# Attention's side work, places for weights and the order of sevens changed in a decoder layer

## The chip, the cores and the metric

The kernel runs on one core of a Trainium2 chip. The metric is the time of one execution on the device in microseconds (us); smaller is better. Engines are named as in the profile: PE (TensorE), DVE (VectorE), ACT (ScalarE), POOL (GpSimd) and SP (SyncE, which here only issues DMAs).

## The reference

One decoder layer over 256 tokens of width 2048, all in float32:

```
x = layer_norm(alpha*x + 0.5*swiglu(x, f1_gu, f1_down))         # feed-forward 1, inner width 5632
mixed = gated(retention(...), sliding_window_attention_sinks(...)) @ w   # token mixers
x = layer_norm(alpha*x + mixed)
x = layer_norm(alpha*x + 0.5*swiglu(x, f2_gu, f2_down))         # feed-forward 2
x = layer_norm(alpha*x + gated per-layer embedding)

def swiglu(x, w_gu, w_down):
    g, u = jnp.split(x @ w_gu, 2, axis=-1)
    return (jax.nn.silu(g) * u) @ w_down
```

The attention has 16 query heads of 64 over 4 key heads, a window of 128 keys, and for each head a learned sink logit in the softmax's denominator. Its gates and inputs come from the columns of one large matrix w_in.

## The kernel before

Every matrix product takes its weights from the chip's memory in chunks of 512 KB and is done in three matmuls: weight and activation are split into a high and a low part, and high x low, high x high and low x high are added (L431, L432, L433). ACT casts the high part of a weight (L105, names with h: hf_gu), DVE subtracts it from the raw one (rf_gu) and so makes the low part (L106, lf_gu). A *unit* is a pair of chunks with the matmuls that use them, of one of these kinds:

- P, plain: 24 matmuls.
- F, Folded: plain, but the low part is made by an accumulating DMA which POOL issues (L170).
- S, a *seven*: seven products of sums of sub-blocks in the place of eight, 21 matmuls. DVE makes the sums u and v of the weights (L226 to L229), ACT and DVE split them (huf, luf, hvf, lvf), and at the end of a block DVE folds the seven products into the results (L541 to L544, in the down product L1059 behind them). The sums of the activations are the *forms* (seven_forms; gaf0 and gaf1 in the gates' part).
- D, Prepared: a seven whose u and v were computed and put in memory earlier, so that it loads six tiles (huf, luf, hvf, lvf, and raw tiles) at once.

All these tiles come from one pool of 46 places (SLOTS). fill(), which is called whenever a unit is done, loads the next unit of the plan or makes the loaded one, if the number of places that slots_for_weights last set is not used up and if less than 90 (far) or 45 (ahead) matmuls are queued in the units at hand. A place count thus decides how long before its use a transfer is issued. Each engine takes its instructions in the order in which the program emits them; SP issues its DMAs in that order too and waits at one whose tile isn't free yet.

Feed-forward 2 computes gate and up in 11 blocks of 512 columns (f20 to f210; loads are named rf2_gu_block_half_number in the order and rf_gu in the profile). The down product has a first and a second half of output columns, each with 22 units whose kinds stand in FIRST_DOWN and SECOND_DOWN; feed-forward 1 uses the same tables. At the end of the second half stand the additions to the residual (L1118) and the layer norm (L646 to L706; lnps at L684 is its transpose on PE).

The attention's scores, softmax and products run as *side work*: side is a list of steps, one of which is run after each chunk of the feature groups (4 chunks each: aqk, akv) and of the gate projection gt (32 chunks of 12 matmuls). For head pair m a step holds one or more parts: att1 (scores as on PE; mask and maxima on DVE), att1b (exponentials on ACT, L1412), att1c (normalising on DVE, L1426), att2 (cutting into wat on ACT, L185), att2a (transposing DMA to mat), att2b (joining into apt on ACT, L201), att3 (ao on PE, L1454, and attt on ACT and DVE). In the profile and the text "head" is such a pair. The list begin holds the step at which head m starts.

Of the kernel before, what the change touches and what calls it, by code (L numbers as in the profile page):

```python
# [9 lines left out]
F32R = mybir.dt.float32r  # L10
# [6 lines left out]
P = 128  # L17
# [24 lines left out]
SEVEN = (0, 1, 2, 3)  # L42

AHEAD = {1: (4, 5), 2: (4,), 3: (4, 5), 4: (4,), 5: (4, 5), 7: (4, 5)}
AHEAD_SLOTS = 32

DELAY = 1

SEVEN_DOWN = (6, 7, 8, 9)

FIRST_DOWN = "PPPPPPFFSFSPSFSPSFSSPS"
SECOND_DOWN = "PPPSPSPSFSPSFSPSPSPPPP"
LEAD = 4

BIG = 3.0e38
# [7 lines left out]
def layer(ctx: ExitStack, tc: tile.TileContext, io):  # L63
# [13 lines left out]
    def banks(name):  # L77
        return [bank(name + str(j)) for j in range(2)]

    def slot(shape, dt, name):  # L80
        return slots.tile(shape, dt, tag="slot", name=name)
# [22 lines left out]
    def split(dst_hi, dst_lo, src, lo_engine=None):  # L104
        act.copy(dst_hi, src)  # L105
        (lo_engine or dve).tensor_tensor(dst_lo, src, dst_hi, ALU.subtract)  # L106
# [249 lines left out]
    def slots_for_weights(n, ahead=45, far=90):  # L356
        room.update(slots=n, ahead=ahead, far=far)
# [136 lines left out]
            if p == sevens[-1]:  # L494
                fold(p1.ap, p6.ap, p7.ap, q5.ap)

    def seven_forms(full, hi, lo, between=None):


        a11, a21 = (full[:, 0::2, t * P : (t + 1) * P] for t in range(2))  # L500
        a12, a22 = (full[:, 1::2, t * P : (t + 1) * P] for t in range(2))
        raw = slot([P, 8, P], F32, "sums")
        f5, f6, f7, f3 = (raw[:, 2 * j : 2 * j + 2, :] for j in range(4))
        dve.tensor_tensor(f5, a21, a22, ALU.subtract)
        dve.tensor_tensor(f7, a11, a21, ALU.subtract)
        dve.tensor_tensor(f6, f5, a11, ALU.subtract)
        dve.tensor_tensor(f3, a12, f6, ALU.add)
        if between is not None:
            between()
        split(hi, lo, raw)  # L510
        return lambda e: [(hi[:, 2 * j + e, :], lo[:, 2 * j + e, :]) for j in range(4)]

    def whole(parts, name):

        full = slot([P, 4, S], F32, name)
        n = 4 // len(parts)
        for j, v in enumerate(parts):
            dve.tensor_tensor(full[:, n * j : n * j + n], v[:, :, :S], v[:, :, S:], ALU.add)
        return full

    def forms_of(parts, name):
        hi, lo = (slot([P, 8, P], F32R, name + w) for w in "hl")
        return seven_forms(whole(parts, name + "w"), hi, lo)
# [338 lines left out]
    ht = big.tile([P, KD, 512], F32R, tag="ht", name="xt")  # L862

    def load_constants():
        act.dma_start(cst, io["cst"])
        act.dma_start(mask, io["mask"])
        act.dma_start(gn, io["gn"])
        act.dma_start(sink, io["att_sinks"].broadcast_to([P, HA]))
# [44 lines left out]
    def gu_units(name, j):  # L913
        if j == 0:
            return [("P", p) for p in range(KD // 2)]
        if name == "f2" and j in AHEAD:
            plain = "P" if j < 4 else "F"
            return units_of(*((f"P{plain}SDSDSP", SEVEN[:3]) if j % 2 else (f"P{plain}SSDSSP", SEVEN)), AHEAD[j])
        order = "FFSSFSSP" if name == "f1" or j > 8 else "PFSSFSSP"
        return units_of(order, SEVEN[: order.count("S")])  # L920

    def gu_keys(name, j):
        return lambda n, p: (name + "_gu", j, n, p)

    def down_units(n_held):
# [4 lines left out]
        first, second = [], []  # L930
        for out, order in ((first, FIRST_DOWN), (second, SECOND_DOWN)):
            n = order.count("S")
# [17 lines left out]
    def ffn(name, i, ht, norm, keep, residual, keepers, away):  # L950
# [4 lines left out]
        made = {}  # L955
# [25 lines left out]
        def convert(g):  # L981
            convert_high(g)()

        for j in range(KF // 4):
            pg, pu = banks(f"{name}g{j}"), banks(f"{name}u{j}")
            units = gu_units(name, j)
            n_of = {(0, 0): KD, (0, 1): KD, (1, 0): KD, (1, 1): KD}
            for kind, p in units:
                if kind in "SD":
                    for at in ((0, 0), (0, 1), (1, 0)):  # L990
                        n_of[at] -= 1
                    n_of[1, 1] -= 2
            sums = [[Sum((pg, pu)[n][t], n_of[t, n]) for n in range(2)] for t in range(2)]
            got = []

            if norm is not None and j == 0:
                front, units = units[:FRONT_PAIRS], units[FRONT_PAIRS:]
                steps = [(gu_keys(name, 0)(n, p), 2 * p, n) for _, p in front for n in range(2)]
                norm.first(steps, rhs, sums, (
                    (3, (1, 0)), (5, "more"), (5, (1, 1)), (7, (0, 2)), (8, (1, 2)), (9, (0, 3)), (10, (1, 3)), (10, "go"),  # L1000
                ))
                slots_for_weights(24)

            def before(u, j=j, offset=KD // 2 - len(units)):
                u += offset
                if j == 0 and norm is None and u % 2 == 0:
                    first_chunk(u // 2)
                    if u == 6:
                        slots_for_weights(24)
                    if u == 2:  # L1010
                        load_constants()
                if j == 0 and u == 7:
                    for g in sorted({p // 2 for p in SEVEN}):
                        hi, lo = (slot([P, 8, P], F32R, f"{name}f{w}{g}") for w in "hl")
                        made[g] = seven_forms(keep[g], hi, lo)
                    if name == "f2":
                        g = AHEAD[1][0] // 2
                        made[g] = forms_of([ht[:, 4 * g : 4 * g + 4, :]], f"{name}f{g}")
                if name == "f2" and j in AHEAD and u == 0:
                    slots_for_weights(AHEAD_SLOTS - j)  # L1020
                if j == KF // 4 - 1 and u in (4, 6):
                    convert(u // 2 - 2)

            block(f"{name}{j}", units, gu_keys(name, j), rhs, forms, sums, lambda *a: got.extend(seven_common(*a)), before)
            if got:
                g, v = got
                for x, ps in ((g, pg), (v, pu)):
                    for t in range(2):
                        dve.tensor_tensor(x[:, t], x[:, t], ps[t], ALU.add)
                act.activation(g, g, AF.Silu)  # L1030
                dve.tensor_tensor(v, g, v, ALU.mult)
            else:
                v = slot([P, 2, 512], F32, f"{name}v{j}")
                for t in range(2):
                    act.activation(v[:, t], pg[t], AF.Silu)
                for t in range(2):
                    dve.tensor_tensor(v[:, t], v[:, t], pu[t], ALU.mult)
            later(1, lambda j=j, v=v: turned(j, v))
# [9 lines left out]
        made = {}  # L1048
# [38 lines left out]
        sums = [[Sum(pn[n][t], n_of[0][t, n]) for n in range(2)] for t in range(2)]  # L1087
# [24 lines left out]
        sums = [[Sum(pt_[t][n], n_of[1][t, n]) for n in range(2)] for t in range(2)]  # L1112
# [74 lines left out]
    def mixers(ht, norm, residual, keepers, away):  # L1187
# [31 lines left out]
        sums = [[Sum(ps[t], KD)] for t in range(2)]  # L1219
# [4 lines left out]
        for c in range(FRONT, KD // 2):  # L1224
            u = take(("w_rv", 0, c))
# [17 lines left out]
        grp = 8  # L1243
# [9 lines left out]
        keep = {}  # L1253
# [92 lines left out]
        for h in range(0, HR, 2):  # L1346
# [3 lines left out]
            g = slot([P, 2, 512], F32, f"rgs{h}")  # L1350
# [3 lines left out]
            c = h // 2  # L1354
# [14 lines left out]
            dst = akv[:, 0:2, :] if j == 4 else aq[j // 2][:, j % 2 * 2 : j % 2 * 2 + 2, :]  # L1369
            rotate(ps, f"ra{j}", dst, *trig["a"], SH_A)  # L1370

        for grp in (20, 16, 17):
            attention_features(grp)
        assert not side

# [87 lines left out]
            return f  # L1463


        begin = [0, 5, 10, 15, 20, 24, 28, 32, 38, 39]
        at = [[] for _ in range(40)]
        for m in range(8):
            for j, part in ((0, att1), (1, att1b), (2, att1c), (3, att2), (4, att2a), (6, att2b)):
                at[begin[m] + j].append(part(m))  # L1470
            at[begin[m + 2]].append(att3(m))
        side.extend((lambda jobs=jobs: [f() for f in jobs]) for jobs in at)

        for grp in (18, 19):
            attention_features(grp)

        made = {}
# [2 lines left out]
        sig = []  # L1480
        for j in range(4):
            def before(c, j=j):
                if c == 0 and j >= 2:
                    g = j - 2
                    made[g] = forms_of([ht[:, 4 * g : 4 * g + 4, :]], f"gaf{g}")

            ps = banks(f"gt{j}")
            paired_out(("w_in_f2", 21 + 2 * j), KD, rhs, ps, before)
            sig.append(slot([P, 2, 512], F32, f"sig{j}"))
            for t in range(2):  # L1490
                (act.copy if j < 2 else dve.tensor_copy)(sig[-1][:, t], ps[t])
# [41 lines left out]
        for b in range(2):  # L1533
# [3 lines left out]
            for n in range(2):  # L1537
                j = 2 * b + n
# [37 lines left out]
        sums = [[Sum(ps[t], KD)] for t in range(2)]  # L1576
# [3 lines left out]
        for c in range(first):  # L1580
            u = take(("w_mix", 3, c))
# [147 lines left out]
    def first_chunk(c):  # L1729

        if c == 0:
            load_x_chunk(0)
            fill()
        if c < 3:
            load_x_chunk(c + 1)
# [157 lines left out]
```

## Time and profile before

| what | value |
|---|---|
| median of 3 runs | 2248.59 us (2248.32 to 2249.66) |
| the profiled execution | 2250.32 us, span 2248.5 us |
| PE busy | 2230.2 us (99%) |
| DVE busy | 1987.0 us (88%) |
| ACT busy | 1421.7 us (63%) |
| mean granted clock of PE | 0.997 |
| transfers issued by SP (queue q1) | 530.16 MB, 70.5% of 16 engines' span |

Busy time is the sum of the durations of an engine's instructions; a wait is the time that an engine stood ahead of an instruction, with what it stood for. In a timeline row the first number is the start, the second the duration, and the brackets hold the idle time ahead of it and what ended that. The granted clock is the share of full speed that the throttle let TensorE have.

### The profile page before, as it was taken

What the parts mean: (1) busy time and instruction counts of PE and PEld (TensorE: products, weight loads), DVE (VectorE), ACT (ScalarE), POOL (GpSimd) and SP (SyncE); (2) the same over time, 40 slices, a digit from 0 to 9 for tenths busy, and PEclk for the clock granted to TensorE, in tenths of its full rate; (3) what the DMA queues carried; (4) which work ended last, traced back from release to release, by engine and by line L of the source; (5) the groups of instructions that cost most, each with busy time, mean ns of one, the idle gap of its engine ahead of it and who ended that gap; (6) DMA issues with size and microseconds to landing.
All of it is one profiled execution on the core that took longest, in us unless ns stands there. A gap on an engine that the chain in (4) does not pass through costs nothing.

```text
span 2248.5 us, 29078 instructions
## 1 busy us (share of the span) xinstructions
PE 2230.2 (99%) x10173; PEld 1846.2 (82%) x10173; DVE 1987.0 (88%) x2601; ACT 1421.7 (63%) x1662; POOL 51.7 (2%) x66
## 2 busy tenths in 40 slices
PE   9999999999999999999999999999999999999998
PEld 8888888888888888888778888888888788888877
DVE  6999999989988898888789778789999899999877
ACT  6777777776554544656766466466667577765533
POOL 0000000000000000000000000000000000000000
PEclk9999999999999999999999999999999999999999
DMA  9989998977686899855657578888889799676872
GB/s 323 252 261 253 248 262 246 266 214 233 235 302 253 304 324 315 272 167 184 197 169 244 165 240 300 299 278 289 309 272 289 254 251 275 207 238 225 290 267 71
DMA packets 294283, 564.48 MB, mean 251 GB/s; under 512 B 92268, under 2 KB 96748, under 8 KB 294136
## 3 DMA queue, kind: packets, MB, share of 16 engines
q1 hardware_dynamic: 283944, 530.16, 70.5%
q0 software_dynamic: 8208, 29.89, 7.1%
q10 hardware_dynamic: 1984, 2.58, 0.4%
q8 instruction: 80, 1.31, 0.2%
q14 instruction: 67, 0.55, 0.1%
HBM read 484.43 MB, written 29.36 MB: 229 GB/s over the span
## 4 chain that ended last, share of the span: by engine, by line
PE 90%; DVE 4%; DMA 3%; issue 2%; ACT 1%; ACTq 0%; POOL 0%; DVEq 0%; POOLq 0%
PE rqk L382 3%; PE f1g L431 3%; PE f1g L432 3%; PE f1g L433 3%; PE f2g L431 2%; PE f2g L432 2%; PE f2g L433 2%; PE f1u L433 2%; PE f1u L431 2%; PE f1u L432 2%; PE f2u L433 2%; PE f2u L431 2%; PE f2u L432 2%; PE aqk L382 2%; PE f1d L433 1%
## 5 line engine op out<-in xcount | busy, mean ns | idle before, releaser
L106 DVE TENSOR_TENSOR lf_gu<-rf_gu,hf_gu 128x1024 fp32r<-128x1024 f32 (+1 forms) x225 | 267.7, 1210 | 21.3 <-ACT hf_gu L105 20.5
L105 ACT CAST hf_gu<-rf_gu 128x1024 fp32r<-128x1024 f32 (+1 forms) x225 | 228.7, 1040 | 35.9 <-DMA rf_gu<-in_f_gu 31.9
L106 DVE TENSOR_TENSOR lw_in_f<-rw_in_f,hw_in_f 128x1024 fp32r<-128x1024 f32 x140 | 167.9, 1220 | 29.8 <-ACT hw_in_f L105 29.8
L106 DVE TENSOR_TENSOR lf_down<-rf_down,hf_down 128x1024 fp32r<-128x1024 f32 x130 | 155.5, 1220 | 14.5 <-ACT hf_down L105 13.9
L105 ACT CAST hf_down<-rf_down 128x1024 fp32r<-128x1024 f32 x130 | 132.8, 1049 | 38.3 <-DMA rf_down<-in_f_down 26.9
L105 ACT CAST huf_gu<-uf_gu 128x1024 fp32r<-128x1024 f32 x76 | 80.1, 1054 | 121.2 <-DVE uf_gu L227 104.0
L105 ACT CAST hw_in_f<-rw_in_f 128x1024 fp32r<-128x1024 f32 x140 | 140.8, 1048 | 8.4 <-PE rv L432 3.2
L105 ACT CAST hvf_gu<-vf_gu 128x1024 fp32r<-128x1024 f32 x76 | 80.1, 1054 | 32.0 <-DVE vf_gu L229 30.2
L106 DVE TENSOR_TENSOR luf_gu<-uf_gu,huf_gu 128x1024 fp32r<-128x1024 f32 x76 | 92.7, 1219 | 0.0
L106 DVE TENSOR_TENSOR lvf_gu<-vf_gu,hvf_gu 128x1024 fp32r<-128x1024 f32 x76 | 92.6, 1219 | 0.0
L431 PE MATMUL f1g<-hf_gu,xt 128*128 128x512 f32 x232 | 90.9, 392 | 0.0
L432 PE MATMUL f1g<-hf_gu,xt 128*128 128x512 f32 x232 | 90.6, 390 | 0.0
L433 PE MATMUL f1g<-lf_gu,xt 128*128 128x512 f32 x232 | 90.5, 390 | 0.0
L431 PE MATMUL f2g<-hf_gu,ht 128*128 128x512 f32 x214 | 83.7, 391 | 0.0
L433 PE MATMUL f2g<-lf_gu,ht 128*128 128x512 f32 x214 | 83.5, 390 | 0.0
L432 PE MATMUL f2g<-hf_gu,ht 128*128 128x512 f32 x214 | 83.5, 390 | 0.0
L433 PE MATMUL f1u<-lf_gu,xt 128*128 128x512 f32 x192 | 74.9, 390 | 0.8 <-DMA lf_gu<-rf_gu 0.8
L170 POOL DMA_DIRECT2D lf_gu<-rf_gu x43 | 37.2, 866 | 1657.5 <-DMA rf_gu<-in_f_gu 1021.6
L431 PE MATMUL f1u<-hf_gu,xt 128*128 128x512 f32 x192 | 74.7, 389 | 0.0
L432 PE MATMUL f1u<-hf_gu,xt 128*128 128x512 f32 x192 | 74.7, 389 | 0.0
L105 ACT CAST huf_down<-uf_down 128x1024 fp32r<-128x1024 f32 x32 | 33.7, 1053 | 57.2 <-DVE uf_down L227 55.2
L433 PE MATMUL f2u<-lf_gu,ht 128*128 128x512 f32 x168 | 65.5, 390 | 0.4 <-DMA lf_gu<-rf_gu 0.4
(1469 smaller groups left out, 6914.7 us busy)
## 6 DMA issues: line engine op xcount, KB each, us to landing
rf_gu<-in_f_gu SPq DMA_DIRECT2D x360, 512.0 KB
rf_down<-in_f_down SPq DMA_DIRECT2D x176, 512.0 KB
rw_in_f<-in_w_in_f SPq DMA_DIRECT2D x148, 512.0 KB
lf_gu<-rf_gu POOLq DMA_DIRECT2D x43, 512.0 KB, 7.5
rw_rv<-in_w_rv SPq DMA_DIRECT2D x32, 512.0 KB
rw_ret<-in_w_ret SPq DMA_DIRECT2D x32, 512.0 KB
rw_mix<-in_w_mix SPq DMA_DIRECT2D x32, 512.0 KB
rw_pg<-in_w_pg SPq DMA_DIRECT2D x32, 512.0 KB
```

Source lines behind the costliest of these rows:

```text
L105: act.copy(dst_hi, src)
L106: (lo_engine or dve).tensor_tensor(dst_lo, src, dst_hi, ALU.subtract)
L170: pool.dma_start(c.lo, c.raw, accum_op=ALU.add)
L382: pe.matmul(ps[f], hi[:, kk, f * P : (f + 1) * P], rhs(k), start=k == 0, stop=k == n_k - 1,)
L431: pe.matmul(o, al, bh, start=first, stop=False)
L432: pe.matmul(o, ah, bh, start=False, stop=False)
L433: pe.matmul(o, ah, bl, start=False, stop=self.left == 0)
```

## The change

Four things change, with the same instructions on every engine:

- In feed-forward 2 the places for weights in blocks 1 to 10 become 36 less the block's number, in every block. Before they were 32 less the number in the blocks of AHEAD (1, 2, 3, 4, 5, 7) and stayed as they were in the others.
- In SECOND_DOWN the last S stands at place 16 in the place of 17 (counted from 0), and two pairs of S are neighbours.
- The attention's side work begins with feature group 17 in the place of 18, over 44 steps in the place of 40, and the parts of one head stand at other distances from its start: 0, 2, 3, 4, 5, 7 in the place of 0, 1, 2, 3, 4, 6. ao of the last head stays in the last step.
- The forms of the gates' part are made in two pieces: the sums at chunk 0 of a gt column, the split at chunk 1 of the loop's numbering. Before both stood at chunk 0.

```diff
-AHEAD_SLOTS = 32
+AHEAD_SLOTS = 36
...
-SECOND_DOWN = "PPPSPSPSFSPSFSPSPSPPPP"
+SECOND_DOWN = "PPPSPSPSFSPSFSSPSPPPPP"
...
-    def seven_forms(full, hi, lo, between=None):
+    def forms_sums(full):
...
+        return raw
+
+    def forms_split(raw, hi, lo):
+
+        split(hi, lo, raw)
+        return lambda e: [(hi[:, 2 * j + e, :], lo[:, 2 * j + e, :]) for j in range(4)]
...
-                if name == "f2" and j in AHEAD and u == 0:
+                if name == "f2" and j and u == 0:
                     slots_for_weights(AHEAD_SLOTS - j)
...
-        for grp in (20, 16, 17):
+        for grp in (20, 16):
             attention_features(grp)
...
-        begin = [0, 5, 10, 15, 20, 24, 28, 32, 38, 39]
-        at = [[] for _ in range(40)]
+        begin = [2, 6, 11, 16, 20, 25, 30, 34, 40, 43]
+        at = [[] for _ in range(44)]
         for m in range(8):
-            for j, part in ((0, att1), (1, att1b), (2, att1c), (3, att2), (4, att2a), (6, att2b)):
+            for j, part in ((0, att1), (2, att1b), (3, att1c), (4, att2), (5, att2a), (7, att2b)):
                 at[begin[m] + j].append(part(m))
             at[begin[m + 2]].append(att3(m))
...
-        for grp in (18, 19):
+        for grp in (17, 18, 19):
             attention_features(grp)
...
-                if c == 0 and j >= 2:
-                    g = j - 2
-                    made[g] = forms_of([ht[:, 4 * g : 4 * g + 4, :]], f"gaf{g}")
+                if j < 2:
+                    return
+                g = j - 2
+                if c == 0:
+                    sums = forms_sums(whole([ht[:, 4 * g : 4 * g + 4, :]], f"gaf{g}w"))
+                    keep["f", g] = sums
+                if c == 1:
+                    hi, lo = (slot([P, 8, P], F32R, f"gaf{g}{w}") for w in "hl")
+                    made[g] = forms_split(keep.pop(("f", g)), hi, lo)
```

SP in feed-forward 2, block 7, before: mf26 is the transposed result of block 6, the rows with 7_0_5 are a Prepared unit's six loads, and 7_0_2 with 7_1_2 is the raw pair of a seven.

```order
L189 DMA_TRANSPOSE mf26_15687<-wf26_15632 128x16x128
L119 DMA rf2_gu_7_0_5_15710<-in_f2_gu 128x2x512
L257 DMA rf2_gu_7_0_5b_15712<-in_f2_gu 128x2x256
L261 DMA huf2_gu_7_0_5_15714<-hudf2_gu_7_0_5_12508 128x1024
L261 DMA luf2_gu_7_0_5_15716<-ludf2_gu_7_0_5_12509 128x1024
L261 DMA hvf2_gu_7_0_5_15718<-hvdf2_gu_7_0_5_12510 128x1024
L261 DMA lvf2_gu_7_0_5_15720<-lvdf2_gu_7_0_5_12511 128x1024
L119 DMA rf2_gu_7_0_2_15750<-in_f2_gu 128x2x512
L119 DMA rf2_gu_7_1_2_15752<-in_f2_gu 128x2x512
```

SP at the same place in the changed kernel:

```order
L119 DMA rf2_gu_7_0_5_15632<-in_f2_gu 128x2x512
L257 DMA rf2_gu_7_0_5b_15634<-in_f2_gu 128x2x256
L261 DMA huf2_gu_7_0_5_15636<-hudf2_gu_7_0_5_12508 128x1024
L261 DMA luf2_gu_7_0_5_15638<-ludf2_gu_7_0_5_12509 128x1024
L261 DMA hvf2_gu_7_0_5_15640<-hvdf2_gu_7_0_5_12510 128x1024
L261 DMA lvf2_gu_7_0_5_15642<-lvdf2_gu_7_0_5_12511 128x1024
L189 DMA_TRANSPOSE mf26_15699<-wf26_15644 128x16x128
L119 DMA rf2_gu_7_0_2_15729<-in_f2_gu 128x2x512
L119 DMA rf2_gu_7_1_2_15731<-in_f2_gu 128x2x512
```

The six loads of unit 7_0_5 moved ahead of the transpose, and the pair 7_0_2 now stands right behind the transpose.

ACT at the end of the attention, before: asc7 are the exponentials of the last head, wat7 and apt7 its cut and joined weights, hw_in_f2_27_7 the last high part of gt, hw_in_f2_29_4 the first of what follows, gaf1h the high part of the forms.

```order
L1412 ACTIVATE asc7_10327,asm7_10357<-asc7_10327,anm7_10334 128x256 x2
L105 CAST hw_in_f2_27_6_10374<-rw_in_f2_27_6_10243 128x1024
L201 COPY apt6_10380<-mat6_10319 128x768 x2
L105 CAST hw_in_f2_27_7_10401<-rw_in_f2_27_7_10270 128x1024
L185 COPY wat7_10407<-asc7_10327 128x768 x2
L105 CAST hw_in_f2_29_4_10422<-rw_in_f2_29_4_10307 128x1024
L105 CAST hw_in_f2_31_4_10444<-rw_in_f2_31_4_10354 128x1024
L105 CAST hw_in_f2_29_5_10460<-rw_in_f2_29_5_10378 128x1024
L1461 CAST attt6_10474<-ao60_10468 64x256
L1461 CAST attt6_10474<-ao61_10469 64x256
L201 COPY apt7_10479<-mat7_10430 128x768 x2
```

ACT at the same place in the changed kernel (its lines are numbered 9 higher from seven_forms on):

```order
L1421 ACTIVATE asc7_10273,asm7_10335<-asc7_10273,anm7_10280 128x256 x2
L105 CAST hw_in_f2_27_5_10352<-rw_in_f2_27_5_10228 128x1024
L201 COPY apt6_10358<-mat6_10302 128x768 x2
L105 CAST gaf1h_10367<-sums_10311 128x1024
L105 CAST hw_in_f2_27_6_10383<-rw_in_f2_27_6_10252 128x1024
L185 COPY wat7_10389<-asc7_10273 128x768 x2
L105 CAST hw_in_f2_27_7_10404<-rw_in_f2_27_7_10300 128x1024
L105 CAST hw_in_f2_29_4_10424<-rw_in_f2_29_4_10332 128x1024
L1470 CAST attt6_10438<-ao60_10432 64x256
L1470 CAST attt6_10438<-ao61_10433 64x256
L105 CAST hw_in_f2_31_4_10455<-rw_in_f2_31_4_10356 128x1024
L201 COPY apt7_10459<-mat7_10410 128x768 x2
```

wat7 moved ahead of hw_in_f2_27_7 and apt7 ahead of hw_in_f2_29_5, each by one weight; gaf1h, which stood ahead of the exponentials of head 7, now stands behind them.

DVE at the end of the second down of feed-forward 2, before: evw and eve are the fold, lw_pg the lows of the next product's weights, f2e00 and f2e01 the last sums.

```order
L106 TENSOR_TENSOR lw_pg_0_2_18770<-rw_pg_0_2_18767,hw_pg_0_2_18769 128x1024
L106 TENSOR_TENSOR lw_pg_0_3_18776<-rw_pg_0_3_18773,hw_pg_0_3_18775 128x1024
L541 TENSOR_TENSOR evw_18782<-eve_18781,f2d1s1_17994 128x512
L542 TENSOR_TENSOR eve_18781<-evw_18782,f2d1s2_17995 128x512
L543 TENSOR_TENSOR evw_18782<-f2d1s3_17996,evw_18782 128x512
L544 TENSOR_TENSOR evw_18782<-f2d1s3_17996,eve_18781 128x512
L1059 SCALAR_TENSOR_TENSOR f2y2_18448<-f2y2_18448,eve_18781 128x1024
L1059 SCALAR_TENSOR_TENSOR f2y3_18496<-f2y3_18496,evw_18782 128x1024
L106 TENSOR_TENSOR lw_pg_0_4_18803<-rw_pg_0_4_18779,hw_pg_0_4_18802 128x1024
L106 TENSOR_TENSOR lw_pg_0_5_18821<-rw_pg_0_5_18806,hw_pg_0_5_18820 128x1024
L1118 TENSOR_TENSOR f2y2_18448<-f2y2_18448,f2e00_17989 128x512
L706 BN_STATS f2st_17009<-f2y2_18448 128x6
```

DVE at the same place in the changed kernel:

```order
L550 TENSOR_TENSOR evw_18744<-eve_18743,f2d1s1_17994 128x512
L551 TENSOR_TENSOR eve_18743<-evw_18744,f2d1s2_17995 128x512
L552 TENSOR_TENSOR evw_18744<-f2d1s3_17996,evw_18744 128x512
L553 TENSOR_TENSOR evw_18744<-f2d1s3_17996,eve_18743 128x512
L1068 SCALAR_TENSOR_TENSOR f2y2_18450<-f2y2_18450,eve_18743 128x1024
L1068 SCALAR_TENSOR_TENSOR f2y3_18496<-f2y3_18496,evw_18744 128x1024
L106 TENSOR_TENSOR lw_pg_0_2_18767<-rw_pg_0_2_18764,hw_pg_0_2_18766 128x1024
L106 TENSOR_TENSOR lw_pg_0_3_18785<-rw_pg_0_3_18770,hw_pg_0_3_18784 128x1024
L106 TENSOR_TENSOR lw_pg_0_4_18803<-rw_pg_0_4_18788,hw_pg_0_4_18802 128x1024
L106 TENSOR_TENSOR lw_pg_0_5_18821<-rw_pg_0_5_18806,hw_pg_0_5_18820 128x1024
L1127 TENSOR_TENSOR f2y2_18450<-f2y2_18450,f2e00_17989 128x512
L715 BN_STATS f2st_17009<-f2y2_18450 128x6
```

The fold and its two L1068 rows moved ahead of lw_pg_0_2 and lw_pg_0_3; the same rows stand ahead of the additions to the residual in both kernels.

More of the change, by code (lines that the diff above doesn't have):

```diff
@@ L507, in seven_forms @@
         dve.tensor_tensor(f3, a12, f6, ALU.add)
+        return raw
+    def forms_split(raw, hi, lo):
+        split(hi, lo, raw)
+        return lambda e: [(hi[:, 2 * j + e, :], lo[:, 2 * j + e, :]) for j in range(4)]
+    def seven_forms(full, hi, lo, between=None):
+        raw = forms_sums(full)
         if between is not None:
             between()
-        split(hi, lo, raw)
-        return lambda e: [(hi[:, 2 * j + e, :], lo[:, 2 * j + e, :]) for j in range(4)]
+        return forms_split(raw, hi, lo)
     def whole(parts, name):
```

## The prediction, made before the changed kernel was run

> **What bounds the kernel now.** I read the page's first part, then the waits of PE, then PE's timeline around the longest waits, and last the windows and the other engines there. The page:
>
> ```profile
> span 2248.5 us, 29078 instructions
> PE 2230.2 (99%) x10173; PEld 1846.2 (82%) x10173; DVE 1987.0 (88%) x2601; ACT 1421.7 (63%) x1662; POOL 51.7 (2%) x66
> ```
>
> TensorE is busy for 99% of the span. The change adds and removes no instruction on any engine, so all that it can give or take lies in the breaks between matmuls. The waits of PE say who ends those breaks (total us, times, longest):
>
> ```profile
> PE ao L1454 <- ACT apt L201: 2.7, 2, 2.4
> PE f27s L433 <- DVE lf_gu L106: 2.1, 1, 2.1
> ...
> PE lnps L684 <- DVE f2y L672: 1.0, 2, 0.6
> PE lnps L684 <- DVE f1y L672: 0.9, 2, 0.5
> PE gt L433 <- DVE lw_in_f L106: 0.8, 1, 0.8
> PE f1u L433 <- DMA lf_gu<-rf_gu: 0.8, 1, 0.8
> PE f27s L433 <- DVE luf_gu L106: 0.8, 1, 0.8
> PE f2u L433 <- DMA lf_gu<-rf_gu: 0.4, 1, 0.4
> ...
> PE f25s L433 <- DVE lvf_gu L106: 0.2, 1, 0.2
> ```
>
> Two places stand out: the last attention head (ao) beside the gate projection (gt), and block 7 of feed-forward 2 (f27s). PE's timeline shows that both cost more than the wait. The first:
>
> ```profile
> 1136.50 0.39 PE L431 MATMUL gt<-hw_in_f,ht 128*128 128x512 f32 x1
> 1136.72 0.39 PE L432 MATMUL gt<-hw_in_f,ht 128*128 128x512 f32 x1
> 1137.90 0.50 PE L433 MATMUL gt<-lw_in_f,ht 128*128 128x512 f32 x1 [0.79 <-DVE lw_in_f L106]
> ...
> 1146.92 0.39 PE L433 MATMUL gt<-lw_in_f,ht 128*128 128x512 f32 x1
> 1149.69 0.66 PE L1454 MATMUL ao<-apt,akv 128*64 128x256 f32 x4 [2.38 <-ACT apt L201]
> ...
> 1150.87 0.63 PE L432 MATMUL ga0a<-hw_in_f,ht 128*128 128x512 f32 x1
> 1151.30 0.63 PE L433 MATMUL ga0a<-lw_in_f,ht 128*128 128x512 f32 x1
> ...
> 1154.24 0.40 PE L431 MATMUL ga0b<-hw_in_f,ht 128*128 128x512 f32 x1
> ```
>
> Undisturbed, a 128x512 matmul starts 0.22 us after the one ahead (1136.50 to 1136.72; over many it is 0.227, and 0.23 is used below). Behind the 2.38 us wait the starts are 0.43 us apart (1150.87 to 1151.30), for eight steps, until 1154.24. The second place:
>
> ```profile
> 1775.29 0.39 PE L432 MATMUL f27s<-hf_gu,ht 128*128 128x512 f32 x1
> 1777.75 0.50 PE L433 MATMUL f27s<-lf_gu,ht 128*128 128x512 f32 x1 [2.07 <-DVE lf_gu L106]
> ...
> 1778.32 0.39 PE L432 MATMUL f27s<-huf_gu,f2fh 128*128 128x512 f32 x1
> 1779.49 0.80 PE L433 MATMUL f27s<-luf_gu,f2fh 128*128 128x512 f32 x1 [0.78 <-DVE luf_gu L106]
> 1780.08 0.63 PE L431 MATMUL f27s<-hvf_gu,f2fl 128*128 128x512 f32 x1
> ...
> 1785.63 0.41 PE L432 MATMUL f2g<-hvf_gu,ht 128*128 128x512 f32 x1
> ```
>
> Here 13 steps take 5.55 us (1780.08 to 1785.63). The windows show both places as a lower granted clock, 0.97 and 0.93 (the third number from the end):
>
> ```profile
> 1150.00:1200.00 50.00, 50.00 (x219) 41.11 (x216) 48.86 (x60) 29.21 (x34) 0.00 (x0) 0.97 0.59 192
> 1750.00:1800.00 50.00, 47.15 (x195) 38.05 (x194) 40.10 (x48) 30.61 (x34) 0.86 (x1) 0.93 0.76 247
> ```
>
> **The change part by part.** *Attention's side work* starts one feature group sooner and its parts stand further apart. A head is a serial chain over four engines. DVE's timeline and the chain of waits show its last links:
>
> ```profile
> 1131.00 1.23 DVE L106 TENSOR_TENSOR gaf1l<-sums,gaf1h 128x1024 fp32r<-128x1024 f32 x1 [1.17 <-ACT gaf1h L105]
> 1139.67 1.23 DVE L106 TENSOR_TENSOR lw_in_f<-rw_in_f,hw_in_f 128x1024 fp32r<-128x1024 f32 x1 [1.82 <-ACT hw_in_f L105]
> ...
> 1143.92 3.69 DMA mat<-wat
> 1147.69 1.96 ACT apt L201 x2
> ```
>
> DVE stands 1.17 us for the cast of gaf1h and 1.82 us for a weight's cast which ACT reaches only behind the exponentials. What is queued behind these on DVE are the weight lows of gt and the normalising of the head, and so gt is late at 1137.90 and ao at 1149.69. Counted back from the last step, on which ao of head 7 stands in both kernels, its scores stood 7 steps earlier and now 9, its exponentials 6 and now 7, the cutting into wat 4 and now 5, the joining into apt 1 and now 2. A step is one chunk of 12 matmuls, 12 x 0.23 = 2.8 us. So the chain as a whole has 2.8 us more, against the 2.38 that were lacking, and the two waits of DVE (1.17 and 1.82) in the same stretch lose their cause besides: gaf1's cast and subtraction now run two chunks behind its sums, and the exponentials have a chunk more to finish behind their maxima. I take the place as cleared. What goes: 1137.90 - 1136.72 - 0.23 = 0.95 at gt, 1149.69 - 1146.92 - 0.23 = 2.54 at ao, 0.3 for the other ao wait (2.7 less 2.4) and 8 x (0.43 - 0.23) = 1.6 at half rate, together **5.4 us**; the bound on the other side, if the same time is lost one step earlier, is 0. The price is that the first head now falls into feature group 17, which ran without side work, and DVE is nearly full there:
>
> ```profile
> 1000.00:1026.00 26.00, 26.00 (x153) 22.56 (x152) 22.94 (x36) 18.78 (x25) 0.00 (x0) 1.00 0.78 261
> ```
>
> ```profile
> 1134.17 1.02 DVE L1390 SCALAR_TENSOR_TENSOR asc<-as,mask 128x384 f32<-128x384 f32 x2
> ...
> 1135.57 0.68 DVE L1392 TENSOR_REDUCE amx<-asc 128x2 f32<-128x512 f32 x1
> ```
>
> Of 26 us 3.06 are free, and masking the scores and their larger maximum alone are 1.7 us of DVE for each head. It fits only while DVE works ahead of PE. I cost it at nothing; without that cover it is a wait of up to 1.7 us, once.
>
> *36 places less the block's number.* Places for weights in blocks 1 to 10 go from 31, 30, 29, 28, 27, 27, 25, 25, 25, 25 to 35, 34 and so on down to 26. In block 7 the late unit is a seven whose raw pair was issued last of a row of loads. The chain of waits, DVE's and SP's timelines:
>
> ```profile
> 1762.44 11.28 DMA rf_gu<-in_f_gu
> ...
> 1773.81 0.69 DVE L226 TENSOR_TENSOR uf_gu<-rf_gu,rf_gu 128x512 f32<-128x512 f32 x1 [8.05 <-DMA rf_gu<-in_f_gu]
> ...
> 1756.26 1.91 SPq L189 DMA_TRANSPOSE mf<-wf  x1
> ```
>
> Between this transpose and the pair (1761.97 on SP) six loads of prepared weights for another unit were sent, 5 x 0.5 + 0.25 = 2.75 MB. DVE idled 8.05 us for the pair, while the unit was 2.07 us late. In the new order the six stand ahead of the transpose, in time that the queue had, and the pair stands right behind the transpose, so it is issued between 1758.2 (1756.26 + 1.91) and 1762. What is late next? At the window's 247 GB/s the pair, 1 MB, is 4.2 us, so it lands by 1766.2 at the latest against 1773.8, that is 7.6 us sooner, against the 2.07 + 0.78 lacking. I take this place as cleared too: 1777.75 - 1775.29 - 0.23 = 2.23, 1779.49 - 1778.32 - 0.23 = 0.94, 1780.08 - 1779.49 - 0.23 = 0.36, 5.55 - 13 x 0.23 = 2.56 at half rate, and 0.2 for f25s, which is the same unit two blocks earlier: **6.3 us**. The low bound is the pair issued no sooner than before and again 11.28 us on the way: nothing is gained then.
>
> *Sevens of the second down.* The last seven ends 24 matmuls sooner (5.5 us), so its fold stands ahead of two weight lows that were ahead of it. But DVE did the fold, all lows and the norm in one unbroken run, and no work leaves that run; the only gain is what DVE is behind PE when the norm starts:
>
> ```profile
> 2135.91 0.39 PE L433 MATMUL f2e<-lf_down,f2ah 128*128 128x512 f32 x1
> 2136.82 0.68 DVE L1118 TENSOR_TENSOR f2y<-f2y,f2e 128x512 f32<-128x512 f32 x1
> ```
>
> The matmul that completes the sum ends at 2136.30 and DVE adds it at 2136.82, 0.5 us behind. The rest of the 1.0 and 0.9 us waits at lnps is the norm's own chain, and stays. I take 0.2 per norm, **0.4 us** for both (0 to 1.0). Two sevens now stand side by side; DVE needs longer for a seven than PE, and the cover is DVE's lead.
>
> Sum: 5.4 + 6.3 + 0.4 = 12.1 us. From the profiled execution of 2250.32 us (1.8 outside the span of 2248.5) that makes 2238.2; it stood 1.7 above the median of the runs, 2248.59, which I forecast from: 2248.59 - 12.1 = **2236.5 us**.
>
> **The rivals.** *One place only moves.* For it speaks the low bound above, and that the attention's chain has 0.4 us to spare if only the 2.8 count. If feed-forward 2 gains nothing, the time is 2236.5 + 6.3 = 2242.8; if attention gains nothing, 2241.9. Against it: both margins have a second source each, DVE's waits of 1.17 and 1.82, and the 7.6 us.
>
> *The half rate stays.* If the slow matmuls are not the waits' doing but a throttle of the stretch, 1.6 + 2.56 = 4.2 us remain: 2240.7. Against it: both times they begin right behind a wait of over 2 us, and behind 0.79 us at 1137.90 none came. [...]
>
> *New waits of the same sum.* Group 17 and the two adjacent sevens each make DVE late by about 2.4 us, which brings the half rate as at 1149.69: 2 x (2.5 + 1.6) = 8 us back, and 0.4 lost: 2245. It holds if DVE's lead over PE is below the 3 us of a head.
>
> *Slower: POOL's accumulations.* In the Folded units PE waits for an accumulating DMA that POOL issues:
>
> ```profile
> lf_gu<-rf_gu POOLq DMA_DIRECT2D x43, 512.0 KB, 7.5
> ```
>
> It takes 7.5 us from issue to landing, and one in block 6 was already 0.4 us late. More places let SP send its 2.75 MB batches and pairs earlier, in blocks 1 to 10, into the stretch in which such a transfer runs. If a batch beside it doubles it to 15, PE waits up to 7.5 us, and at half rate thereafter, 2.6 more as in f27: 10 us. With two such blocks the time is 2236.5 + 20 = 2256.5; it decides from a wait of 5.7 us in each of two, since 2 x (5.7 + 2.6) = 16.6 = 12.1 + 4.5. [...] Against the rival: 41 of the 43 were in time, and the two waits were 0.8 and 0.4 us.
>
> **How the numbers follow.** Both places cleared: 0.50, at 2236.5, 2233 to 2239 (3.5 below: 0.6 more from the norms, 0.4 from f2u, the 1.3 by which the runs differ, and 1.2 for short breaks that no row above names; 2.5 above: a fifth of both places stays). One place only moves: 0.22, 2239 to 2243.5. The half rate stays: 0.05, 2240.7. New waits of the same sum: 0.11, 2243.5 to 2253. Slower: 0.12. The range from 2233 to 2243.5 takes in the first two. 0.2%, 4.5 us, is about what a measurement of this kernel can tell from no change: faster is below 2244.1 and slower above 2253.1. That gives 0.78, 0.10 and 0.12.
>
> **What would show it.** Right: no PE wait of ao on apt and none of f27s on DVE above 0.3 us; a granted clock of 1.00 in the windows where it was 0.97 and 0.93; the pair of f27 landing before 1767 on the old scale; lnps waits between 0.6 and 1.0 in sum each. Wrong: a wait of PE on aq or as while group 17 to 19 are multiplied; PE waits on an accumulating DMA above 1 us; or slow matmuls that stay without a wait ahead of them.

## The result and the profile after

| | before | changed |
|---|---|---|
| median of 4 runs | 2248.45 us (2247.37 to 2249.66) | 2233.73 us (2233.44 to 2234.82) |
| profiled execution | 2250.32 us, span 2248.5 | 2234.82 us, span 2233.0 |

The ratio is 0.9935, 95% interval 0.9918 to 0.9952: 14.7 us faster, where 12.1 were forecast (2236.5). The head of the page and the waits of PE after the change (total us, times, longest):

```profile
span 2233.0 us, 29081 instructions
PE 2222.8 (100%) x10173; PEld 1842.0 (82%) x10173; DVE 1987.0 (89%) x2601; ACT 1421.2 (64%) x1662; POOL 51.7 (2%) x66
...
PE f1e L431 <- DVE evw L550: 0.8, 1, 0.8
PE mr1s L433 <- DVE luw_ret L106: 0.8, 1, 0.8
PE f1u L433 <- DMA lf_gu<-rf_gu: 0.4, 1, 0.4
```

No wait on apt, on f27s, on lw_in_f or at lnps is left among them. The same number of matmuls takes 7.4 us less of busy time (2230.2 to 2222.8), about 4.2 us of it because those at half rate at the two places are gone too (the prediction's 1.6 and 2.56). The windows of the two places:

```profile
1100.00:1150.00 50.00, 50.00 (x244) 39.27 (x243) 38.50 (x68) 34.87 (x57) 0.00 (x0) 1.00 0.61 182
1150.00:1200.00 50.00, 50.00 (x222) 41.39 (x222) 49.45 (x60) 28.34 (x32) 0.00 (x0) 1.00 0.58 190
1750.00:1800.00 50.00, 50.00 (x222) 41.42 (x221) 45.63 (x54) 34.97 (x39) 1.72 (x2) 1.00 0.90 254
```

The clock is 1.00 in each, and PE is busy for all 50 us. Where the time came from shows best when the start of the same matmul (by its number in PE's order) is compared in both traces. From one such point to the next the changed kernel gained or lost, in us:

| stretch | changed against before |
|---|---|
| feed-forward 1, gate and up (f1u on POOL's DMA and around the start) | -0.68 |
| feed-forward 1, end of the first down (f1e on evw) | +0.80 |
| feed-forward 1, norm behind the second down | -1.39 |
| attention and gt | -5.79 |
| retention's mixing and its norm | +0.64 |
| feed-forward 2, block 5 (f25s) | -0.50 |
| block 6 (f2u on POOL's DMA) | -0.69 |
| block 7 (f27s) | -6.31 |
| end of the first down | -0.25 |
| norm behind the second down | -1.42 |
| the rest | +0.20 |
| all | -15.39 |

In block 7, SP's and DVE's timelines of the changed kernel:

```profile
1745.99 4.99 SPq L189 DMA_TRANSPOSE mf<-wf  x1
1753.31 14.71 SPq L119 DMA_DIRECT2D rf_gu<-in_f_gu  x12
...
1760.01 0.69 DVE L226 TENSOR_TENSOR uf_gu<-rf_gu,rf_gu 128x512 f32<-128x512 f32 x1 [2.83 <-DMA rf_gu<-in_f_gu]
```

The pair is issued at 1753.31, and DVE starts on it 6.7 us later, against 11.84 before (1761.97 to 1773.81). The changed kernel is 7.4 us ahead at this matmul, so on the old scale these are 1760.7 and 1767.4. In the row of 1753.31 the pair are the first two of the twelve loads.

### The profile page after: what moved, and what is told of

The parts are those of the page before. It is cut to its first block, busy times and chain, and to the rows that moved or that the text cites. A ratio compares the mean times of both kernels' runs of the same rounds, so it can differ in the third digit from the quotient of the medians.

```text
span 2233.0 us, 29081 instructions
## 1 busy us (share of the span) xinstructions
PE 2222.8 (100%) x10173; PEld 1842.0 (82%) x10173; DVE 1987.0 (89%) x2601; ACT 1421.2 (64%) x1662; POOL 51.7 (2%) x66
## 4 chain that ended last, share of the span: by engine, by line
PE 94%; DVE 2%; DMA 2%; issue 1%; ACT 1%; ACTq 0%; POOL 0%; DVEq 0%; POOLq 0%
PE f2g L433 3%; PE f2g L432 3%; PE f2g L431 3%; PE rqk L382 3%; PE f1g L433 2%; PE f1g L431 2%; PE f1g L432 2%; PE f2u L433 2%; PE f2u L431 2%; PE f2u L432 2%; PE f1u L433 2%; PE f1u L431 2%; PE f1u L432 2%; PE aqk L382 2%; PE f2d L433 1%; PE f1e L431 1%
## 5 line engine op out<-in xcount | busy, mean ns | idle before, releaser
L431 PE MATMUL f2u<-hf_gu,ht 128*128 128x512 f32 x168 | 65.7, 391 | 0.0
```

The source lines that it names most:

```text
L431: pe.matmul(o, al, bh, start=first, stop=False)
```

## The experiments

Twelve kernels ran in three groups, each beside executions of before, which had medians of 2248.17, 2247.95 and 2248.34 us. Single executions of one kernel differ by up to 6.5 us, so the stretches of the profiles say more than the medians about where time goes.

**Each part alone.** e1_side takes the begins, the 44 steps, group 17 and the distances; e2_forms only the cut of the forms; e3_places and e4_down one line each:

```diff
-AHEAD_SLOTS = 32
+AHEAD_SLOTS = 36
-                if name == "f2" and j in AHEAD and u == 0:
+                if name == "f2" and j and u == 0:
```

```diff
-SECOND_DOWN = "PPPSPSPSFSPSFSPSPSPPPP"
+SECOND_DOWN = "PPPSPSPSFSPSFSSPSPPPPP"
```

> Only the side work's schedule changed (group 17, 44 steps, the other distances), the forms as before. Theory, the chain is too short by a step: both ao waits go and with them the half-rate matmuls, 4.5 us faster than before; the wait of gt on lw_in_f (0.95) stays in part, since DVE still stands for the cast of gaf1h. Rival, the burst of the forms is the whole cause: ao stays late by 1 us or more and the gain is under 2 us.

> Only the forms of the gates' part cut in two, the split two chunks behind the sums. Theory, the chain is too short: DVE's wait of 1.17 us for gaf1h goes and the gt wait of 0.95 us with it, ao on apt is still waited for by 1.2 us or more, 1 to 2.5 us faster than before. Rival, the burst is the whole cause: no ao wait above 0.3 us is left, 5 us or more faster.

> Only the places in feed-forward 2 changed (36 less the block's number in every block). Theory, the late raw pair of block 7 was held behind six loads: the waits of f27s and f25s and the half rate go, 6.8 to 7.5 us faster than before with the 0.5 us of the accumulating DMA in block 6 among it. Rival, the places alone do not do it since feed-forward 2 inherits an earlier state from the attention: under 5 us faster.

> Only the order of sevens in the second down changed. Theory, two weight lows leave DVE's unbroken run ahead of the norm: the lnps waits of f1y and f2y both go, 2.8 us faster than before. Rival, the norms' waits went because of something else in the changed kernel: under 1 us faster, as the prediction's 0.4 had it.

| kernel | median us | ratio to before (interval) | stretch that it touches |
|---|---|---|---|
| e1_side | 2241.14 | 0.9973 (0.9963 to 0.9982) | attention -5.79 |
| e2_forms | 2244.87 | 0.9984 (0.9976 to 0.9993) | attention -4.11 |
| e3_places | 2242.49 | 0.9974 (0.9965 to 0.9984) | f27s -6.31, f25s -0.50, f2u -0.69 |
| e4_down | 2245.52 | 0.9988 (0.9979 to 0.9997) | norms -1.39 and -1.83 |

Places and sevens do what the theory said of them at the matmuls named; in the median the places gave 5.7 us, less than the 6.8 to 7.5 expected, and the sevens 2.7. Of the places' gains the -0.50 is not theirs, though: f25s has it in e4_down too, and in five more profiles with the old places, so its wait in the profile before was one of that execution. Block 6's f2u is another matter. It loses its 0.69 in all five profiles with the new places (the changed kernel's, e3_places, e9_first, e12_noforms, e13_shift), and of the seven with the old ones in e1_side alone; and behind block 7, where before happened to lose nothing to POOL's DMAs, most of those seven lose 0.9 to 1.8 us, and the five nothing. Side and forms do not add: each alone clears most of the attention's 5.79 us, and e1_side clears all of it, the gt wait too, which I had expected to stay. e2_forms fits neither theory: its gain (3.3 us in the median, 4.11 in the attention) was above the 2.5 that the first allowed, since no slow matmuls followed (behind the wait of 1.63 us they start 0.24 us apart, 1147.95 to 1148.19), but an ao wait stayed:

```profile
PE ao L1463 <- ACT apt L201: 1.6, 1, 1.6
```

**What in the side work.** e8_begin takes the new begins and steps with the old distances; e10_begin_forms adds the cut of the forms to that; e11_dist takes the new distances alone:

```diff
-            for j, part in ((0, att1), (1, att1b), (2, att1c), (3, att2), (4, att2a), (6, att2b)):
+            for j, part in ((0, att1), (2, att1b), (3, att1c), (4, att2), (5, att2a), (7, att2b)):
```

> Before with the new begins and 44 steps, but the old distances of a head's parts (0, 1, 2, 3, 4, 6), and the forms uncut: the last head's apt is joined three steps ahead of ao. Theory, what lacked is the distance between a head's end and ao: no ao wait above 0.3 us, 5 us or more of the attention's 5.8 us gone. Rival, exponentials one step behind the scores make ACT and DVE stand for each other, and that makes weights late: the gt wait on lw_in_f stays at 0.5 us or more.

> Before with the new begins and 44 steps, the old distances, and now the forms cut in two. With the forms uncut the wait of ao turned into one of gt on ACT's hw_in_f of 2.2 us and one on lw_in_f of 0.7. Theory, that wait has two cures, the distance of the exponentials or the cut of the forms, since both take a wait of ACT and DVE for each other out of one stretch: the gt waits fall below 0.5 us in sum and the attention gains 5 us or more against before. Rival, only the distance cures it: a gt wait of 1.5 us or more stays, and the attention gains under 2 us.

> Before with the new distances of a head's parts (0, 2, 3, 4, 5, 7) alone: old begins, 40 steps, forms uncut, so that the last head's apt is joined in the very step of its ao. Theory, distances without an earlier begin leave the chain too short at its end: the gt wait of 0.95 us goes, the ao wait grows from 2.4 to 3 us or more, and the time is within 2 us of before or slower. Rival, the distances are the cure by themselves: ao waits for under 1 us and the attention gains 4 us or more.

e8_begin has a median of 2249.46 (ratio 1.0005, 0.9996 to 1.0014): no gain at all, and 0.6 us in the attention's stretch. Its ao wait is gone, but PE waits elsewhere. The waits of PE and the timelines of PE, ACT and DVE there:

```profile
PE gt L431 <- ACT hw_in_f L105: 2.2, 1, 2.2
...
1136.29 0.50 PE L431 MATMUL gt<-hw_in_f,ht 128*128 128x512 f32 x1 [2.22 <-ACT hw_in_f L105]
...
1134.25 1.04 ACT L105 CAST gaf1h<-sums 128x1024 fp32r<-128x1024 f32 x1 [3.09 <-DVE sums L507]
1135.20 1.04 ACT L105 CAST hw_in_f<-rw_in_f 128x1024 fp32r<-128x1024 f32 x1
...
1135.32 1.23 DVE L106 TENSOR_TENSOR gaf1l<-sums,gaf1h 128x1024 fp32r<-128x1024 f32 x1 [1.11 <-ACT gaf1h L105]
```

ACT stands 3.09 us for the sums of gaf1, with the next weight's cast queued behind; DVE stands 1.11 us for ACT's answer. The wait on lw_in_f is still 0.7 us, as the rival had it. e10_begin_forms, where that pair is cut, has 2243.75 (0.9982, 0.9973 to 0.9991), no wait in the attention and -5.59 there, as its theory had it. e11_dist has 2243.30 (0.9978, 0.9969 to 0.9988), -4.95, and this wait:

```profile
PE ao L1454 <- ACT apt L201: 0.8, 1, 0.8
```

So e11's theory fell and its rival held: with apt joined in the very step of its ao, PE waits 0.8 us for it, not 3. What made the chain late was not first its distance from the end but ACT and DVE standing for each other in one stretch. Spreading the distances or cutting the forms takes most of it away; the earlier begin adds the last 0.8 us (5.79 of e1_side less 4.95), and by itself only moves the wait.

> The changed kernel with the forms of the gates' part uncut, as in before. Theory, once begins and distances are new, the cut has nothing left to gain: no PE wait on apt, hw_in_f or lw_in_f above 0.3 us, within 1 us of the changed kernel, 14 to 15.5 us faster than before. Rival, each of the parts carries its share: gt waits for 0.5 us or more, 1 to 3 us slower than the changed kernel.

e12_noforms has 2233.48 us (0.9940, 0.9927 to 0.9953), as fast as the changed kernel, with -5.79 in the attention: the cut of the forms is not needed beside the rest. The three other parts alone gave 7.0 (e1_side), 5.7 and 2.7 us, together 15.4, against its 14.9: within what the medians can tell, they add.

**What in the places.** e6_block7:

```diff
-                if name == "f2" and j in AHEAD and u == 0:
-                    slots_for_weights(AHEAD_SLOTS - j)
+                if name == "f2" and j in (*AHEAD, 8) and u == 0:
+                    slots_for_weights({7: 29, 8: 25}.get(j, AHEAD_SLOTS - j))
```

> Before with 29 places in the place of 25 in block 7 of feed-forward 2 alone (25 again from block 8 on), which puts the six loads of unit 7_0_5 ahead of the transpose and the raw pair 7_0_2 right behind it, as in the changed kernel. Theory, the pair was late for what stood ahead of it: both waits of f27s go and with them the half rate, the profile's loss around f27 falls from 6.3 to under 0.5 us, the median is 4.5 to 6.3 us lower; f25s and the accumulating DMA of block 6 stay as they were. Rival, the places of blocks 1 to 6 matter by giving DVE and ACT a lead: f27s still waits for 1 us or more.

2243.53 us (0.9979, 0.9968 to 0.9989), 4.4 us faster, just short of the 4.5 expected. Block 7 loses its whole 6.31 us, with no wait of f27s. Four places in one block are what counts for it. In this profile another wait was larger than in before:

```profile
PE lnps L684 <- DVE f2y L672: 2.6, 2, 2.2
```

In the profiles with the old second down that wait ranges from 0.4 (e10_begin_forms) through 1.0 (before) to 2.6 us; in those with the new order it does not appear.

**What in the order of sevens.** e7_pair:

```diff
-SECOND_DOWN = "PPPSPSPSFSPSFSPSPSPPPP"
+SECOND_DOWN = "PPPSPSPSFSPSFSSPPSPPPP"
```

> Before with two neighbouring sevens in the second down at places 13 and 14, as in the changed kernel, but the last seven at place 17, as before. Theory, the last seven's place decides, since it frees tiles and lets loads of the last plain units come before DVE's unbroken run: PE still waits at lnps for f1y and f2y, 0.6 us or more in sum each, and the time is within 1 us of before. Rival, any earlier end of the middle sevens does it: both lnps waits under 0.3 us, 2 to 3 us faster.

The changed order has one pair of neighbouring sevens, at places 13 and 14, not two. e7_pair, which has it too, runs in 2247.52 us (0.9998, 0.9989 to 1.0007): no gain. For f2y the theory holds; f1y's wait is shorter than the 0.6 us it asked, but it is 0.3 to 0.4 in e1_side, e6_block7, e8_begin and e11_dist too, where the second down is as before:

```profile
PE lnps L684 <- DVE f2y L672: 1.6, 2, 1.2
PE lnps L684 <- DVE f1y L672: 0.3, 1, 0.3
```

Beside the pair, the last seven's place is what decides: e4_down differs from e7_pair in it alone. Moving it without the pair was not tried. The gain suggests the same for the first down, whose order ends in a seven and whose fold PE waits for (f1e on evw). e9_first and e13_shift change FIRST_DOWN in the changed kernel:

```diff
-FIRST_DOWN = "PPPPPPFFSFSPSFSPSFSSPS"
+FIRST_DOWN = "PPPPPPFFSFSSFSPSFSPSSP"    # e9_first
+FIRST_DOWN = "PPPPPFFSFSPSFSPSFSSPSP"    # e13_shift
```

> The changed kernel with another order of FIRST_DOWN, PPPPPPFFSFSSFSPSFSPSSP: the last seven is followed by a plain unit (24 matmuls, 5.4 us) in the place of none, so that the fold's reading of its banks is over before the next half starts. Theory, the second down's gain can be had in the first down too: the wait of f1e on evw (0.8 us in the profile after, 0 to 1.1 elsewhere) and that of f2e go, 0.5 to 1.5 us faster than the changed kernel, about 15.5 to 16 us faster than before. Rival, the moved sevens make DVE late elsewhere in the first down: new PE waits on lows of the down weights, no gain or a loss against the changed kernel.

> The changed kernel with FIRST_DOWN as PPPPPFFSFSPSFSPSFSSPSP: the old order one place sooner, the plain unit so saved at the end, so that no unit's load comes later than before and the last seven is followed by 24 plain matmuls. Theory, the waits of f1e and f2e on evw go (0.8 and 0 us in the profile after, up to 1.1 in others) without the late accumulating DMA that the other order brought: 0.3 to 1.5 us faster than the changed kernel, 15 to 16 us faster than before. Rival, the first sevens, one place sooner, find their forms or sums late: a new wait at the start of the first down, no gain.

e9_first has 2236.45 us (0.9949 to before, 0.9937 to 0.9962), 2.7 above the changed kernel's median. evw is no longer waited for, but the Folded unit that now stands behind two sevens is, in both feed-forwards:

```profile
PE f1d L433 <- DMA lf_down<-rf_down: 1.7, 1, 1.7
PE f2d L433 <- DMA lf_down<-rf_down: 1.4, 1, 1.4
```

e13_shift keeps every unit's distance to its load. It has 2232.89 us (0.9936, 0.9923 to 0.9949), and its profile (span 2229.5) the fewest waits of PE:

```profile
PE f1g L431 <- ACT hf_gu L105: 0.5, 1, 0.5
PE pln L1681 <- DVE plnst L1679: 0.2, 1, 0.2
PE mr1s L433 <- DVE lvw_ret L106: 0.2, 1, 0.2
```

The two waits on evw are gone (0.5 and 0.6 in e12_noforms of the same group). Its five runs, 2231.32 to 2235.20, overlap the 2233.08 to 2235.18 of e12_noforms: that it beats the changed kernel is likely by the profile and not shown by the times.

## Why the prediction was right, and where not

2233.73 us lies in the range forecast for both places cleared (2233 to 2239), near its lower end. By the profile that is owed mostly to the sevens, which gave 2.4 us more than the sum had for them, where the range allowed 0.6.

- *Attention, 5.4 forecast, 5.79 measured.* The waits named and the half rate behind them went, and nothing came in feature group 17: no wait on aq or as. The reason was half right. I counted the 2.8 us of an added chunk first and DVE's waits of 1.17 and 1.82 "besides"; e8_begin and e11_dist show the reverse. The 1.6 us at half rate in the sum came in part by luck: of the five profiles with the attention as before, four have it, but e6_block7 waits nearly the same 2.36 us for apt with no slow matmul behind it, and its stretch is 1.54 us shorter (see the last section).
- *Places, 6.3 forecast (6.1 of it at f27s), 6.31 measured at f27s and 0.69 at f2u.* f27s went by the mechanism stated (e6_block7). That the size came out is partly luck, since it is that of one execution: with the old places and no part of the change there, f27s cost 3.1 to 4.9 us in e1_side, e2_forms, e4_down, e7_pair, e8_begin, e10_begin_forms and e11_dist, mostly for want of some or all of the slow matmuls. e3_places is 5.7 faster in the median all the same; by the profiles that is because POOL's DMAs are in time in feed-forward 2 (no wait of f2u there; 0.4 us in before, 1.2 in e4_down, 2.0 in e8_begin). The sum had left these as they were. The 0.2 for f25s was no effect of the change.
- *Sevens, 0.4 forecast, 2.81 measured.* This is the term that was mis-sized, by the step "no work leaves that run". DVE's timeline, before and after:

```profile
2120.35 3.79 DVE L106 TENSOR_TENSOR lf_down<-rf_down,hf_down 128x1024 fp32r<-128x1024 f32 x3 [2.33 <-ACT hf_down L105]
```

```profile
2105.01 1.23 DVE L106 TENSOR_TENSOR lf_down<-rf_down,hf_down 128x1024 fp32r<-128x1024 f32 x1 [0.22 <-ACT hf_down L105]
2108.32 1.23 DVE L106 TENSOR_TENSOR lf_down<-rf_down,hf_down 128x1024 fp32r<-128x1024 f32 x1 [2.09 <-ACT hf_down L105]
...
2121.44 0.68 DVE L1127 TENSOR_TENSOR f2y<-f2y,f2e 128x512 f32<-128x512 f32 x1
```

The unbroken run began behind an idle 2.33 us with three lows of the down weights; now it begins with one. The other two are made ahead of the idle time: SP has sent its last ten loads of the down weights 26.0 us ahead of lnps (2100.92 to 2126.92), before it was 24.7 (2116.94 to 2141.67). L1118 moved 1.4 us ahead of PE's place: before, 4.85 us lay between its start and lnps at 2141.67, of which PE had lost 0.77 waiting; after, 5.48 (2121.44 to 2126.92, without a wait). So the rest of the waits at lnps, which I had called the norm's own chain, went too. The second error was the bound of 0.5 us: I took the wrong matmul as the one that completes the sum. In the changed trace that matmul is

```profile
2121.93 0.39 PE L433 MATMUL f2e<-lf_down,f2ah 128*128 128x512 f32 x1
```

and DVE had begun to add at 2121.44, ahead of it.

- *The rivals.* "One place only moves" is what e8_begin alone would have been. "The half rate stays" fell: no slow matmul is left at either place. "New waits of the same sum" did not come: PE waits neither in feature group 17 nor behind the two adjacent sevens. The accumulating DMAs were waited for less, not more, though their median from issue to landing rose a little (7.5 to 7.9 us).
- *The signs.* Two missed. DVE starts on the pair of f27 at 1767.4 on the old scale, where it was to land before 1767: it took about 6.7 us from issue to landing, where I had worked out 4.2. The waits at lnps, which were to be 0.6 to 1.0 in sum each, are gone. The signs on ao, f27s and the granted clock came as stated.
- *Not foreseen:* f1e on evw (+0.80) and retention's luw_ret (+0.64). The change does not touch them, and both vary as much between the other profiles (f1e 0 to 1.1, luw_ret 0 to 0.8); they are put down to that, which was not tested.

## What to carry to other kernels

Where two in-order engines answer each other (a maximum, an exponential, a normalising), put the halves of each question a step apart before moving the whole chain earlier: an earlier begin alone moved the wait to the next work in the queue. For a late transfer look at what is queued ahead of it, and give space in the one block where that matters. When a run of work on an engine seems unbroken, ask what could be done in the idle time just ahead of it, and which loads would have to come for that. Slow matmuls behind a wait can be there in one execution and not in the next (before and e6_block7, behind 2.4 us for ao each): forecast them apart from the wait.

## What the runs showed of the hardware

In these runs the half rate did not follow from the length of a wait alone. In e4_down block 7 waits nearly as in before (1.70 and 0.78 us, there 2.07 and 0.78), and PE's timeline behind it has no slow step (0.24 us from 1777.43 to 1777.67, where before had 0.43):

```profile
1775.35 0.50 PE L433 MATMUL f27s<-lf_gu,ht 128*128 128x512 f32 x1 [1.70 <-DVE lf_gu L106]
...
1777.09 0.50 PE L433 MATMUL f27s<-luf_gu,f2fh 128*128 128x512 f32 x1 [0.78 <-DVE luf_gu L106]
1777.43 0.40 PE L431 MATMUL f27s<-hvf_gu,f2fl 128*128 128x512 f32 x1
1777.67 0.40 PE L432 MATMUL f27s<-hvf_gu,f2fh 128*128 128x512 f32 x1
```

In block 7 of before 13 slow steps came behind these waits, and the granted clock from 1750 to 1800 us is 0.93; in e4_down and e2_forms, with 1.7 and 1.8 us and 0.8 behind, it is 1.00.

In before the clock was at 0.50 for 3.4 us behind the wait for ao (1150.77 to 1154.18), and for 6.8 us in block 7 (1778.83 to 1785.65). The rows below are stretches around a wait, first of before and of e6_block7 (both for ao), then of e1_side and of e4_down (both for f27s):

```profile
1147.36:1150.77 3.41, 1.08 (x9) 0.78 (x10) 1.97 (x4) 3.21 (x5) 0.00 (x0) 1.00 0.99 356
1150.77:1154.19 3.42, 3.42 (x9) 2.66 (x9) 3.33 (x6) 2.12 (x4) 0.00 (x0) 0.50 0.72 242
```

```profile
1144.69:1148.10 3.41, 2.33 (x11) 1.56 (x9) 3.41 (x4) 3.22 (x5) 0.00 (x0) 1.00 1.01 211
1148.10:1151.51 3.41, 2.13 (x14) 1.59 (x15) 1.95 (x3) 3.31 (x6) 0.00 (x0) 1.00 0.98 347
1151.51:1154.93 3.42, 3.42 (x17) 2.81 (x16) 3.35 (x6) 1.12 (x2) 0.00 (x0) 1.00 0.49 172
```

```profile
1766.82:1770.23 3.41, 1.19 (x4) 0.71 (x5) 3.41 (x5) 3.08 (x3) 0.00 (x0) 1.00 1.05 398
1770.23:1773.64 3.41, 3.41 (x9) 2.45 (x9) 3.10 (x3) 3.41 (x5) 0.00 (x0) 0.50 1.04 386
```

```profile
1771.92:1775.33 3.41, 1.74 (x8) 1.12 (x6) 3.34 (x6) 2.24 (x4) 0.00 (x0) 1.00 1.05 392
1775.33:1778.75 3.42, 2.46 (x8) 1.45 (x9) 3.42 (x4) 3.42 (x4) 0.00 (x0) 1.00 1.05 386
1778.75:1782.16 3.41, 3.41 (x16) 2.81 (x16) 3.10 (x4) 3.41 (x5) 0.00 (x0) 1.00 1.04 384
```

The first number behind the comma is PE's busy time; the rest of the stretch PE stood idle. The granted clock is the third number from the end. In before PE is idle for 2.33 us, and the next row has a clock of 0.50; in e6_block7 it is idle for 1.08 and 1.28 us, 2.36 in all, and the clock stays at 1.00. In e1_side 2.22 us are followed by a row at 0.50, in e4_down 1.67 and 0.96, 2.63 in all, by one at 1.00. So in each couple the longer idle time is the one with no slow matmul behind it. What decides between them was not shown.
